# A two-block transformer kernel on one core: low part of the experts' gates by ScalarE, another place for the expert tiles, a fourth weight-row buffer

## The chip, the core and the metric

The kernel runs on one core of a Trainium2 chip. The metric is the device time of one execution in microseconds, smaller is better. A core has TensorE (PE in the profile; its weight loads are PEld), VectorE (DVE), ScalarE (ACT), GpSimd (POOL), and SyncE (SP), whose queue issues nearly all of the DMAs here.

## What is computed

The input is 256 tokens of width 1024. A first block of two layers is followed by a second block of two layers. Each layer of the first block has a mixer (attention, convolution and recurrence), then a mixture of 16,384 experts, then a gated per-layer embedding (PLE). The change lies in the experts' part, and its other edits touch what all parts share:

```python
def peer(xn, w_q, sub_keys, u, v):
    q = (xt @ w_q).reshape(t, 8, 2, 128)
    sc = jnp.einsum('thpc,pnc->thpn', q, sub_keys)
    top_s, top_i = lax.top_k(sc, 16)
    ...
    expert = i1 * 128 + i2                  # 8 heads x 16 experts for each token
    gate = jax.nn.softmax(best_s, axis=-1)
    act = jax.nn.gelu(jnp.einsum('cd,chkd->chk', xc, u[ec]))
    return jnp.einsum('chk,chkd->cd', gc * act, v[ec])
...
h = h + peer(rmsnorm(h, norm_ffn[l]), ...)
ple_gate = jax.nn.sigmoid(rmsnorm(h, norm_ple[l]) @ w_ple_gate[l])
h = h + ple_gate * (p[l] @ w_ple_proj[l])
```

## The kernel before

Nothing is gathered. For all 16,384 experts the kernel computes the product of the tokens with u (128 rows of experts on the partitions, 256 tokens as columns), applies gelu, multiplies by a dense table of gates that is zero for an expert that a token did not choose, and multiplies with v. The table `act` is [128, 128, 256] in float32, 128 KB of each partition. One step over u is a block `b` of 256 experts (64 blocks in a layer): four DMAs of 256 KB bring its rows into a `raw` buffer, VectorE turns them (L894, two transposes into `ut`) and TensorE makes 16 matmuls of 256 columns (L898). These matmuls in float32 stand in the trace as 32 records to a block. `u_split` is another form of this step, which the later blocks use: it turns the rows in place (L906) and splits them into a high and a low part. `u_out` applies gelu on ScalarE (L924, L927) and multiplies by the gates where they are already there (L925).

While the first u blocks run, the routing (scores, best 16, softmax of the gates) works on VectorE. Then comes the sweep, `spread_gates`, which builds the dense table for four tokens at a time: 64 groups in a layer, four of them to a block of u (`SWEEP_STEPS`). A group is

- `oh` (L859) and `eq` (L861): two comparisons of 128x512 on VectorE that give the one-hot rows of both halves of the expert's number. `oh` has two buffers, `eq` one.
- `rhs` (L863): one VectorE multiplication of 128x1024, `eq` times the gates `gp`. `gp` has two float16 parts, high and low, so that the sum of both holds the float32 gate. `rhs` has four buffers.
- 8 matmuls of 128x128 (L868): 4 tokens by two parts, into one PSUM bank out of three in turn.
- The evacuation: VectorE multiplies the experts for which u is already done (L872), ScalarE copies the other rows (L874).

After the sweep the v stage (`v_pair`) runs, in which TensorE does 24 matmuls of 512 columns for a pair of 128-expert rows (L943). Their stationary operands `ah` and `al` take over the buffers of `rhs` (same tag), their moving ones are the split rows of v, `whi` and `wlo`. Some of the u blocks run between them. The PLE follows; the load of its input p, `praw` (L993 is its transpose on TensorE), and the reload of `h` stand in SP's queue among the loads of its weights.

All rows of weights go through the ring of `raw` buffers (8 KB of a partition each, three of them). ScalarE rounds a part of them to `whi` (L167), and VectorE makes the rest `wlo` (L170), three buffers each, which TensorE reads. The order of each engine's instructions is set by the framework's scheduler, which walks the program by priorities and the buffers that are free: `K.ahead()` raises the priority of loads, `GPRIO` that of the sweep's matmuls. So another count of buffers or another duration of a step gives another order.

`SHIFTS` puts small unused tiles ahead of others, and thus moves what is allocated behind them. The entry "peer" puts 64 bytes of each partition between `act` and the tiles of the sweep.

Of the kernel before, what the change touches and what calls it, by code (L numbers as in the profile page):

```python
# [12 lines left out]
F32 = mybir.dt.float32  # L13
# [3 lines left out]
FP16 = mybir.dt.float16  # L17
U32 = mybir.dt.uint32
AF = mybir.ActivationFunctionType
ALU = mybir.AluOpType  # L20
# [4 lines left out]
S = 256  # L25
# [9 lines left out]
URGENT = 3000  # L35
SHIFTS = {"zp": (0, 288), "zp2": (384, 384), "ple": (384, 128), "peer": (64, 64)}
SQ_ACT = (2, 5, 7)
# [14 lines left out]
class Ctx:  # L52
# [21 lines left out]

    def shift(self, pool, size, name="shift"):

        if size:
            pool.tile([128, size // 4], F32, name=name, bufs=1)
# [78 lines left out]
    def raw_tile(self):  # L157
        return self.ring.tile([128, 2048], F32, name="raw", tag="raw", bufs=3)

# [515 lines left out]
GT = 4  # L675
GSCALE = 32768.0
# [9 lines left out]
def peer(K, a, l, pre, xg, row, pool, ctx):  # L686
# [8 lines left out]
    tc, nc = K.tc, K.nc  # L695
# [25 lines left out]
    nT = pool.tile([128, S], FP16, name="nT")  # L721
    gp = pool.tile([128, 2, S], FP16, name="gp")
    sc_b = [scratch([128, 4, 128]) for _ in range(2)]
# [82 lines left out]
    def routing():  # L806
# [24 lines left out]
        for src, dst in ((m_f, mT), (e_f, nT), (best_v.rearrange("p b h k -> p b (h k)"), None)):  # L831
# [3 lines left out]
            if dst is not None:  # L835
                nc.scalar.activation(dst, ps[:, 0:S], AF.Copy)
            else:
                rest = m_f.rearrange("p b n -> p (b n)")
                nc.scalar.activation(gp[:, 0], ps[:, 0:S], AF.Copy, scale=GSCALE)
                nc.vector.scalar_tensor_tensor(gp[:, 1], ps[:, 0:S], GSCALE, gp[:, 0], op0=ALU.mult,  # L840
                                               op1=ALU.subtract)
            yield
# [3 lines left out]
    def spread_gates():  # L846
# [5 lines left out]
        for i, t0 in enumerate(range(0, S, GT)):  # L852
# [8 lines left out]
            nc.vector.tensor_tensor(eq, io4, tok(nT), ALU.is_equal)  # L861
            rhs = pool.tile([128, 2, 128, GT], FP16, name="rhs", tag="rhs", bufs=4)
            nc.vector.tensor_tensor(rhs, eq[:, None].to_broadcast([128, 2, 128, GT]),  # L863
                                    gp[:, :, None, ts].to_broadcast([128, 2, 128, GT]), ALU.mult)
            with tc.high_priority(offset=GPRIO):
                for t in range(GT):
                    for part in range(2):
                        nc.tensor.matmul(pg[:, t], oh[:, :, t], rhs[:, part, :, t], start=t + part == 0,  # L868
                                         stop=t == GT - 1 and part == 1)
            pg = pg.rearrange("p t n -> p n t")  # L870
# [963 lines left out]
```

## Time and profile before

| | |
|---|---|
| three runs | 3617.34, 3620.2, 3631.05 us (median 3620.2) |
| profiled execution, its own time | 3630.35 us |
| its span in the trace | 3628.6 us |
| mean granted clock of TensorE | 0.975 |
| PE busy | 3484.8 us (96%) |
| PE weight loads busy | 3187.9 us (88%) |
| DVE busy | 2623.3 us (72%) |
| ACT busy | 1475.1 us (41%) |
| POOL busy | 604.2 us (17%) |
| sweep of layer 0, sweep of layer 1 | about 604 to 784 us, about 1922 to 2104 us |

The engines work side by side, so busy shares do not add up. "Granted clock" is the share of full speed at which TensorE was allowed to run, and a stretch at half of it lasts twice as long for the same matmuls. Where one engine waits, a row names the instruction that released it, after an arrow. "SPq" is SP's queue, with the DMAs that it issues.

### The profile page before, as it was taken

The page shows a single profiled execution, that of the slowest core. Times are in us where ns is not written, and L with a number is a line of the kernel's source. Part 1 is how long each engine was busy: PE and PEld are TensorE (multiplying, and loading weights), DVE is VectorE, ACT ScalarE, POOL GpSimd, SP SyncE. Part 2 cuts the span into 40 slices and gives each one's busy share as a digit, 9 for nine tenths or more (in the row PEclk, how much of TensorE's full clock was granted, in tenths as well). Part 3 has the DMA queues.
Part 4 walks back from the last instruction along what each step waited for, and adds up shares of the span by engine and source line. Part 5 has one row for each costly group of instructions (what it writes and reads, how often), then busy time and mean ns, then how long its engine had stood idle before and what let it go on. Part 6 is the DMA issues. An engine that isn't in the chain of part 4 may idle for free. (4 is left out here: it accounts for less than half of the span.)

```text
span 3628.6 us, 60192 instructions
## 1 busy us (share of the span) xinstructions
PE 3484.8 (96%) x23381; PEld 3187.9 (88%) x23381; DVE 2623.3 (72%) x4704; ACT 1475.1 (41%) x2418; POOL 604.2 (17%) x583
## 2 busy tenths in 40 slices
PE   8999998999999999999999999999989999999999
PEld 8898887888888889998888888888789899988999
DVE  6967668876666568775668866666578877698775
ACT  6455111234444446553112144444445344444434
POOL 1200111000000012101120000000033543345441
PEclk9999999999999999999999999999989999999999
DMA  7775756436666567765765346665666534665433
GB/s 178 180 187 140 164 128 139 93 94 189 184 184 187 196 156 173 196 159 147 155 138 113 94 130 190 188 189 186 190 151 141 109 85 116 164 129 120 96 85 126
DMA packets 433976, 541.70 MB, mean 149 GB/s; under 512 B 28665, under 2 KB 392219, under 8 KB 432667
## 3 DMA queue, kind: packets, MB, share of 16 engines
q1 hardware_dynamic: 433690, 537.86, 58.5%
q8 instruction: 183, 3.00, 0.4%
q14 instruction: 103, 0.84, 0.1%
HBM read 530.39 MB, written 6.32 MB: 148 GB/s over the span
## 5 line engine op out<-in xcount | busy, mean ns | idle before, releaser
L170 DVE TENSOR_TENSOR wlo<-raw,whi 128x1024 fp32r<-128x1024 f32 x670 | 862.7, 1293 | 325.8 <-ACT whi L167 311.3
L167 ACT ACTIVATE whi<-raw 128x1024 fp32r<-128x1024 f32 x696 | 728.7, 1051 | 709.0 <-PE mm L199 271.9
L898 PE MATMUL mm<-x,ut 128*128 128x256 f32 x2368 | 542.6, 386 | 1.2 <-ACT act L927 1.2
L200 PE MATMUL mm<-x,wlo 128*128 128x256 f32 x1760 | 506.6, 288 | 14.4 <-DVE wlo L170 14.1
L898 PEld LDWEIGHTS mm<-x,ut 128*128 128x128 f32 x2368 | 453.0, 194 | 64.3 <-ACT act L927 3.9
L198 PE MATMUL mm<-x,whi 128*128 128x256 f32 x1760 | 504.4, 287 | 3.3 <-ACT whi L167 3.3
L199 PE MATMUL mm<-x,whi 128*128 128x256 f32 x1708 | 488.9, 286 | 0.0
L200 PE MATMUL gg<-x,wlo 128*128 128x256 f32 (+1 forms) x1456 | 410.5, 282 | 9.3 <-DVE wlo L170 9.1
L198 PE MATMUL gg<-x,whi 128*128 128x256 f32 (+1 forms) x1456 | 410.9, 282 | 4.9 <-ACT whi L167 4.9
L199 PE MATMUL gg<-x,whi 128*128 128x256 f32 x1400 | 393.6, 281 | 1.3 <-DVE x L303 1.3
L200 PEld LDWEIGHTS mm<-x,wlo 128*128 128x128 f32 x1760 | 340.8, 194 | 18.2 <-DVE wlo L170 17.2
L198 PEld LDWEIGHTS mm<-x,whi 128*128 128x128 f32 x1760 | 340.7, 194 | 10.7 <-issue 5.6
L199 PEld LDWEIGHTS mm<-x,whi 128*128 128x128 f32 x1708 | 331.6, 194 | 1.9 <-issue 0.7
L943 PE MATMUL ax<-wlo,ah 128*128 128x512 f32 x1024 | 323.0, 396 | 2.6 <-DVE wlo L170 2.6
L943 PE MATMUL ax<-whi,al 128*128 128x512 f32 x1024 | 321.4, 395 | 0.0
L200 PEld LDWEIGHTS gg<-x,wlo 128*128 128x128 f32 (+1 forms) x1456 | 276.3, 190 | 11.7 <-DVE wlo L170 11.3
L943 PE MATMUL ax<-whi,ah 128*128 128x512 f32 x1024 | 286.6, 395 | 0.0
L198 PEld LDWEIGHTS gg<-x,whi 128*128 128x128 f32 (+1 forms) x1456 | 275.7, 189 | 8.2 <-ACT whi L167 5.6
L894 DVE STREAM_TRANSPOSE ut<-raw 128x1024 f32<-128x1024 f32 x148 | 181.9, 1236 | 130.8 <-DMA raw<-in_peer_u_dram 114.1
L199 PEld LDWEIGHTS gg<-x,whi 128*128 128x128 f32 x1400 | 265.9, 190 | 3.5 <-DVE x L303 1.4
L943 PEld LDWEIGHTS ax<-wlo,ah 128*128 128x128 f32 x1024 | 190.2, 187 | 54.8 <-DVE wlo L170 9.2
L943 PEld LDWEIGHTS ax<-whi,al 128*128 128x128 f32 x1024 | 191.7, 187 | 47.1
(534 smaller groups left out, 6593.5 us busy)
## 6 DMA issues: line engine op xcount, KB each, us to landing
raw<-in_w_in_dram SPq DMA_DIRECT2D x592, 256.0 KB
raw<-in_peer_u_dram SPq DMA_DIRECT2D x512, 256.0 KB
raw<-in_peer_v_dram SPq DMA_DIRECT2D x128, 1024.0 KB
raw<-in_w_branch_dram SPq DMA_DIRECT2D x16, 1024.0 KB
raw<-in_w_out_dram SPq DMA_DIRECT2D x16, 1024.0 KB
raw<-in_w_peer_q_dram SPq DMA_DIRECT2D x64, 256.0 KB
raw<-in_w_in_dram SPq DMA_DIRECT2D x64, 128.0 KB
raw<-in_w_branch_dram SPq DMA_DIRECT2D x32, 256.0 KB
```

Of the source, the lines that this page charges most:

```text
L167: nc.scalar.activation(view(hi), src, AF.Copy)
L170: (nc.gpsimd if pool else nc.vector).tensor_tensor(view(lo), src, view(hi).bitcast(F32), ALU.subtract)
L198: t.matmul(out, wh, xh, start=start, stop=False)
L199: t.matmul(out, wh, xl, start=False, stop=False)
L200: t.matmul(out, wl, xh, start=False, stop=stop)
L894: nc.vector.transpose(turned[jh], blk)
L898: nc.tensor.matmul(ps[:, jh], turned[jh][:, k].rearrange("p j c -> p (j c)"), xs[:, k], start=k + jh == 0, stop=k == KT - 1 and jh == 1)
L943: nc.tensor.matmul(out[tb][c], lhs[:, j, ts], r[:, c * 512:c * 512 + 512], start=b + j == 0 and lhs is ah and r is vh, stop=b == 63 and j ...
```

## The change

There are four edits.

1. The gates. `gp` now holds the high part alone, and a new tile `gl` the low part in float32. The multiplication by the gates is two steps: VectorE writes the high half of `rhs` (128x512 in place of 128x1024), and ScalarE writes the low half, with one activation of 128x128 for each of the four tokens, scaled by a column of `gl`. This half is now stored token by token, so that the matmul reads 128 elements that lie side by side. The matmuls are as many as before. VectorE's next `eq` must wait until ScalarE has read the one buffer of `eq`.
2. `SHIFTS["peer"]` becomes (0, 0). With this, and with `gp` 512 bytes smaller and `gl` 1024 bytes bigger, `oh`, `eq`, `rhs` (so `ah` and `al` too) and what follows lie 448 bytes further on, beside a common shift of 4096.
3. `raw` has four buffers in place of three (8 KB more).
4. The scratch for DMA descriptors is 4096 bytes in place of 8192.

```diff
-SHIFTS = {"zp": (0, 288), "zp2": (384, 384), "ple": (384, 128), "peer": (64, 64)}
+SHIFTS = {"zp": (0, 288), "zp2": (384, 384), "ple": (384, 128), "peer": (0, 0)}
...
-        return self.ring.tile([128, 2048], F32, name="raw", tag="raw", bufs=3)
+        return self.ring.tile([128, 2048], F32, name="raw", tag="raw", bufs=4)
...
-    gp = pool.tile([128, 2, S], FP16, name="gp")
+    gp = pool.tile([128, S], FP16, name="gp")
+    gl = pool.tile([128, S], F32, name="gl")
...
-                nc.scalar.activation(gp[:, 0], ps[:, 0:S], AF.Copy, scale=GSCALE)
-                nc.vector.scalar_tensor_tensor(gp[:, 1], ps[:, 0:S], GSCALE, gp[:, 0], op0=ALU.mult,
-                                               op1=ALU.subtract)
+                nc.scalar.activation(gp, ps[:, 0:S], AF.Copy, scale=GSCALE)
+                nc.vector.scalar_tensor_tensor(gl, ps[:, 0:S], GSCALE, gp, op0=ALU.mult, op1=ALU.subtract)
...
             eq = pool.tile([128, 128, GT], FP16, name="eq", tag="eq", bufs=1)
             nc.vector.tensor_tensor(eq, io4, tok(nT), ALU.is_equal)
-            rhs = pool.tile([128, 2, 128, GT], FP16, name="rhs", tag="rhs", bufs=4)
-            nc.vector.tensor_tensor(rhs, eq[:, None].to_broadcast([128, 2, 128, GT]),
-                                    gp[:, :, None, ts].to_broadcast([128, 2, 128, GT]), ALU.mult)
+            rhs = pool.tile([128, 2, 128 * GT], FP16, name="rhs", tag="rhs", bufs=4)
+            hi = rhs[:, 0].rearrange("p (n t) -> p n t", t=GT)
+            lo = rhs[:, 1].rearrange("p (t n) -> p t n", t=GT)
+            nc.vector.tensor_tensor(hi, eq, tok(gp), ALU.mult)
+            for t in range(GT):
+                nc.scalar.activation(lo[:, t], eq[:, :, t], AF.Copy, scale=gl[:, t0 + t:t0 + t + 1])
             with tc.high_priority(offset=GPRIO):
                 for t in range(GT):
-                    for part in range(2):
-                        nc.tensor.matmul(pg[:, t], oh[:, :, t], rhs[:, part, :, t], start=t + part == 0,
-                                         stop=t == GT - 1 and part == 1)
+                    nc.tensor.matmul(pg[:, t], oh[:, :, t], hi[:, :, t], start=t == 0, stop=False)
+                    nc.tensor.matmul(pg[:, t], oh[:, :, t], lo[:, t], start=False, stop=t == GT - 1)
...
-    nc = _bacc.Bacc("TRN2", target_bir_lowering=False, num_devices=1, dynamic_dma_scratch_size=8192)
+    nc = _bacc.Bacc("TRN2", target_bir_lowering=False, num_devices=1, dynamic_dma_scratch_size=4096)
```

The change also moves instructions, at places that the diff does not show. In the rows that follow, the lines of the kernel after lie up to three further on than before: L859 is now L860, L861 is L862, L863 is L866, L872 is L875, L874 is L877, L894 is L897, L906 is L909. "x2" stands for two like instructions in a row.

The first place is the beginning of layer 0's sweep, on VectorE, from the first multiplication by the gates on. Before:

```order
L863 TENSOR_TENSOR rhs<-eq,gp 128x1024
L861 TENSOR_TENSOR eq<-io_4654,nT 128x512
L863 TENSOR_TENSOR rhs<-eq,gp 128x1024
L894 STREAM_TRANSPOSE ut<-raw 128x1024
L861 TENSOR_TENSOR eq<-io_4654,nT 128x512
L863 TENSOR_TENSOR rhs<-eq,gp 128x1024
L861 TENSOR_TENSOR eq<-io_4654,nT 128x512
L863 TENSOR_TENSOR rhs<-eq,gp 128x1024
L894 STREAM_TRANSPOSE ut<-raw 128x1024
L872 SCALAR_TENSOR_TENSOR act<-act,gg 128x38x4
L859 TENSOR_TENSOR oh<-io_4654,mT 128x512
```

The same place on VectorE after:

```order
L866 TENSOR_TENSOR rhs<-eq,gp 128x512
L862 TENSOR_TENSOR eq<-io_4653,nT 128x512
L897 STREAM_TRANSPOSE ut<-raw 128x1024
L866 TENSOR_TENSOR rhs<-eq,gp 128x512
L862 TENSOR_TENSOR eq<-io_4653,nT 128x512
L866 TENSOR_TENSOR rhs<-eq,gp 128x512
L875 SCALAR_TENSOR_TENSOR act<-act,gg 128x38x4
L860 TENSOR_TENSOR oh<-io_4653,mT 128x512
L862 TENSOR_TENSOR eq<-io_4653,nT 128x512
L897 STREAM_TRANSPOSE ut<-raw 128x1024
L875 SCALAR_TENSOR_TENSOR act<-act,ax 128x38x4
L860 TENSOR_TENSOR oh<-io_4653,mT 128x512
```

Three groups' multiplications, no longer four, now stand ahead of the first evacuation, and the fourth group's comes only behind a transpose, a further evacuation and an `oh`. On ScalarE, at the same place after, the new activations stand between those that were there (L877 evacuations, L927 and L930 gelu):

```order
L841 ACTIVATE gp<-ax 128x256
L868 ACTIVATE rhs<-eq,gl 128x128 x12
L877 ACTIVATE act<-gg 128x90x4
L927 ACTIVATE mm<-mm 128x2x32
L868 ACTIVATE rhs<-eq,gl 128x128 x4
L877 ACTIVATE act<-ax 128x90x4 x2
```

The second place is the end of layer 0's sweep, on VectorE, where the first block of `u_split` has its two transposes. Before:

```order
L863 TENSOR_TENSOR rhs<-eq,gp 128x1024
L861 TENSOR_TENSOR eq<-io_4654,nT 128x512
L906 STREAM_TRANSPOSE raw<-raw 128x8x4x32 x2
L863 TENSOR_TENSOR rhs<-eq,gp 128x1024
L894 STREAM_TRANSPOSE ut<-raw 128x1024
L872 SCALAR_TENSOR_TENSOR act<-act,gg 128x64x4
L859 TENSOR_TENSOR oh<-io_4654,mT 128x512
L861 TENSOR_TENSOR eq<-io_4654,nT 128x512
L872 SCALAR_TENSOR_TENSOR act<-act,ax 128x64x4
L859 TENSOR_TENSOR oh<-io_4654,mT 128x512
L894 STREAM_TRANSPOSE ut<-raw 128x1024
L863 TENSOR_TENSOR rhs<-eq,gp 128x1024
```

The same place on VectorE after:

```order
L866 TENSOR_TENSOR rhs<-eq,gp 128x512
L897 STREAM_TRANSPOSE ut<-raw 128x1024
L862 TENSOR_TENSOR eq<-io_4653,nT 128x512
L909 STREAM_TRANSPOSE raw<-raw 128x8x4x32 x2
L875 SCALAR_TENSOR_TENSOR act<-act,ax 128x62x4
L860 TENSOR_TENSOR oh<-io_4653,mT 128x512
L866 TENSOR_TENSOR rhs<-eq,gp 128x512
L875 SCALAR_TENSOR_TENSOR act<-act,gg 128x62x4
L860 TENSOR_TENSOR oh<-io_4653,mT 128x512
L897 STREAM_TRANSPOSE ut<-raw 128x1024
L862 TENSOR_TENSOR eq<-io_4653,nT 128x512
```

The two transposes come about half a block of u earlier (the evacuation beside them has 62 rows of experts, before 64), and behind them stand an evacuation and an `oh` at once, where a multiplication and a transpose of 1.24 us came first.

The third place is SP's queue where layer 0's PLE begins. Before:

```order
L95 DMA raw<-in_peer_v_dram 128x2x1024 x21
L95 DMA raw<-in_w_ple_proj_dram 128x2x1024
L95 DMA raw<-in_w_ple_gate_dram 32x2x1024 x12
L95 DMA h<-h_store 128x2048
L95 DMA praw<-in_p_dram 128x2x256
L95 DMA raw<-in_w_ple_gate_dram 32x2x1024 x4
```

The same place on SP after:

```order
L96 DMA raw<-in_peer_v_dram 128x2x1024 x21
L96 DMA raw<-in_w_ple_proj_dram 128x2x1024
L96 DMA raw<-in_w_ple_gate_dram 32x2x1024 x16
L96 DMA h<-h_store 128x2048
L96 DMA praw<-in_p_dram 128x2x256
L96 DMA raw<-in_w_in_dram 32x8x256 x32
```

The last four loads of the gate's weights, 1 MB in all, have moved ahead of the loads of `h` and `praw`. In the same way four loads of `w_in` stand between the first two loads of norm vectors at the program's start, where they came behind all ten of these before. On the whole the other engines' orders differ from before in few places outside the sweep.

## Rows read from the trace of the kernel before

**Rows 1.** Busy time by stretch: both sweeps; columns in the first line.

```profile
core 0: us, PE busy (x) PEld busy (x) DVE busy (x) ACT busy (x) POOL busy (x), PEclk, DMA share, GB/s
604.00:784.00 180.00, 173.31 (x1006) 152.57 (x1006) 148.38 (x303) 38.14 (x95) 0.00 (x0) 0.96 0.39 91
1922.00:2104.00 182.00, 174.55 (x1008) 153.62 (x1007) 148.72 (x303) 38.24 (x95) 0.00 (x0) 0.95 0.39 90
```

**Rows 2.** PE's waits from 604 to 784: us, times, longest.

```profile
PE ax L868 <- DVE oh L859: 4.2, 3, 2.0
PE gg L868 <- DVE rhs L863: 1.6, 1, 1.6
```

**Rows 3.** PE's waits from 1922 to 2104, same columns.

```profile
PE ax L868 <- DVE oh L859: 4.9, 3, 2.8
```

**Rows 4.** Groups of VectorE, 604 to 784: count, busy us, mean ns, idle before.

```profile
L863 DVE TENSOR_TENSOR rhs<-eq,gp 128x1024 f16<-128x1024 f16 x64 | 43.7, 683 | 1.1
L894 DVE STREAM_TRANSPOSE ut<-raw 128x1024 f32<-128x1024 f32 x28 | 34.8, 1243 | 11.8 <-PE mm L898 7.9 <-DMA raw<-in_peer_u_dram 3.6
L861 DVE TENSOR_TENSOR eq<-io,nT 128x512 f16<-128x512 f16 x64 | 26.5, 413 | 0.8
L872 DVE SCALAR_TENSOR_TENSOR act<-act,ax 128x160 f32<-128x160 f32 (+15 forms) x42 | 15.0, 368 | 11.5 <-PE ax L868 11.3
```

**Rows 5.** A group of ScalarE, 604 to 784, same columns.

```profile
L874 ACT ACTIVATE act<-ax 128x352 f32<-128x352 f32 (+15 forms) x42 | 17.1, 420 | 62.8 <-DVE act L872 62.8
```

**Rows 6.** ScalarE by line: duration ns min/median/max, first and last start, form.

```profile
L1467 ACT ACTIVATE ddh<-packed,gt x64: 382/388/403, 2799.0 to 3458.7; 128x128 fp32r<-128x128 f32 x64
L302 ACT ACTIVATE x<-h,v_norm_mix x40: 491/497/512, 10.2 to 3146.0; 128x256 fp32r<-128x256 f32 x40
```

**Rows 7.** Timeline from the start: start us, length us, instruction, [idle before].

```profile
10.18 3.30 ACT L302 ACTIVATE x<-h,v_norm_mix 128x256 fp32r<-128x256 f32 x8
...
16.45 2.01 ACT L167 ACTIVATE whi<-raw 128x1024 fp32r<-128x1024 f32 x2 [2.36 <-DMA raw<-in_w_in_dram]
...
17.56 0.58 PE L198 MATMUL gg<-x,whi 128*128 128x256 f32 x1 [1.62 <-ACT whi L167]
```

**Rows 8.** Timeline, beginning of layer 0's sweep.

```profile
612.16 1.11 PE L868 MATMUL ax<-rhs,oh 128*128 128x128 f16 x8 [1.53 <-DVE oh L859]
```

**Rows 9.** Timeline, layer 0: a wait inside the sweep, then its end.

```profile
704.06 2.06 PE L868 MATMUL ax<-rhs,oh 128*128 128x128 f16 x16 [0.65 <-DVE oh L859]
...
755.90 2.37 DVE L906 STREAM_TRANSPOSE raw<-raw 128x1024 f32<-128x1024 f32 x2 [3.13 <-DMA raw<-in_peer_u_dram]
...
760.22 0.41 DVE L859 TENSOR_TENSOR oh<-io,mT 128x512 f16<-128x512 f16 x1
...
760.69 1.11 PE L868 MATMUL ax<-rhs,oh 128*128 128x128 f16 x8 [1.97 <-DVE oh L859]
...
763.42 0.88 PE L868 MATMUL gg<-rhs,oh 128*128 128x128 f16 x6 [1.62 <-DVE rhs L863]
```

**Rows 10.** Busy time by stretch, columns as in Rows 1: behind waits of PE.

```profile
613.50:621.00 7.50, 7.11 (x35) 5.56 (x33) 7.29 (x20) 2.34 (x5) 0.00 (x0) 0.55 0.53 116
705.50:710.00 4.50, 4.50 (x18) 3.77 (x16) 4.12 (x10) 1.01 (x3) 0.00 (x0) 0.62 0.71 146
...
764.00:768.00 4.00, 3.99 (x15) 3.15 (x14) 3.86 (x10) 0.94 (x3) 0.00 (x0) 0.62 0.72 255
...
2082.00:2088.00 6.00, 5.99 (x20) 4.73 (x20) 5.79 (x13) 0.94 (x3) 0.00 (x0) 0.50 0.50 175
```

**Rows 11.** The same, for two stretches of the mixers.

```profile
160.00:260.00 100.00, 98.97 (x842) 97.83 (x841) 73.98 (x184) 50.64 (x78) 4.57 (x2) 1.00 0.75 191
1500.00:1600.00 100.00, 100.00 (x873) 97.31 (x872) 68.67 (x122) 49.51 (x88) 3.56 (x2) 1.00 0.68 178
```

**Rows 12.** The same, line L943 alone: only PE, PEld, clock, DMA.

```profile
1200.00:1300.00 100.00, 100.00 (x430) 80.14 (x429) 1.00 0.56 188
```

**Rows 13.** PE's waits over the whole span, columns as in Rows 2.

```profile
PE mm L993 <- DMA praw<-in_p_dram: 14.2, 2, 8.5
```

## The prediction, made before the changed kernel had run

> **What bounds the kernel now.** I read the busy times by stretch first, since the change works mostly in the two sweeps. There TensorE is busy 173.31 of 180 us and 174.55 of 182 us, VectorE 148.38 and 148.72, ScalarE 38.14 and 38.24 [rows 1]. A sweep has 64 groups, so a group takes 173.31/64 = 2.71 us of TensorE (its own matmuls and a quarter of a block of u), 2.32 us of VectorE and 0.60 us of ScalarE. TensorE is the bound, VectorE is close behind, ScalarE has room. The reader is to see that lighter work for VectorE can win only the time in which TensorE waits for it. That is 6.7 us in the first sweep and 7.45 us in the second (180 or 182 less busy time), and most of it is for `oh` or `rhs`: 4.2 and 1.6 us, and 4.9 us for `oh` in the second [rows 2, 3].
>
> The second thing that a wait costs is the clock. Behind the waits TensorE's granted clock falls from full speed (2.4 GHz) towards half of it (1.2 GHz): 0.55 over 7.5 us, 0.62 over 4.5 us, 0.62 over 4 us in layer 0 [rows 10]. What is lost is the length times one minus the clock. Over whole sweeps that is 180 x 0.04 = 7.2 us and 182 x 0.05 = 9.1 us [rows 1]. So the most that the sweeps can give back is 6.7 + 7.45 + 7.2 + 9.1 = 30 us of 3630, or 0.8%.
>
> **The gates' multiplication, steady part.** VectorE's step of 128x1024 took 683 ns, and its steps of 128x512 take 413 ns [rows 4]. The change makes the first into one of the second kind: 64 x 0.27 = 17.3 us less VectorE time in each sweep, 131 us in place of 148. This lies beside TensorE's 173 us and is worth nothing by itself.
>
> What it adds is four activations of 128x128 a group on ScalarE. No such step is in the trace of before. The nearest row is a 128x128 activation with a multiplier that differs by partition, 388 ns [rows 6]. One of 128x256 takes 497 ns alone [rows 6], but eight in a row take 3.30 us, 0.41 us each [rows 7]. So one overlaps the next by 0.09 us, and I take 0.30 us each in a row and 0.39 apart. That is 1.2 to 1.55 us a group, 77 to 99 us a sweep. ScalarE goes from 38 to 115 to 137 us, still under 173.
>
> The cost is in the chain, since `eq` has one buffer: `eq` (0.41), a hand-over (`oh` ended at 760.63 and TensorE began at 760.69, 0.06 us [rows 9]), four activations (1.2 to 1.55), a hand-over, the next `eq`. That is 1.73 to 2.08 us. If ScalarE has one other step in front, as its evacuation of 0.42 us [rows 5], it is 2.15 to 2.5 us. All this is below 2.71 us, so TensorE should stay the bound; the other VectorE steps (transpose, `oh`, the evacuation) stand between one `eq` and the next and hide part of it. I take 0 for the steady part.
>
> The Trainium skill speaks against this edit: "ScalarE: Activation LUTs", in Rules for kernel authors, says to use VectorE and not ScalarE for multiplications, VectorE being up to about three times faster in 16-bit types. No run here shows that ratio for this step. By that rule, if ScalarE's time counted in full, the edit would cost and not gain; the second rival is this case.
>
> **The beginning of the sweep.** Before, TensorE waited 1.53 us for the fourth group's `oh` [rows 8]; the fourth multiplication was done long before. After, that multiplication stands behind a transpose (1.24 us [rows 4]), an evacuation (0.37) and an `oh` (0.41). Walking the new order with these durations, the fourth group is ready some 0.7 us later than before, and each of the next two groups has a wait of about 1 us where it had little or none, while the first groups lose nothing. So TensorE arrives at its next ten matmuls of u 1 to 1.6 us later. For both layers I take **+3 us**, with 0 and +4 as ends.
>
> **The end of the sweep.** Two transposes of `u_split` waited 3.13 us for their DMA and ended at 758.27 [rows 9]. Behind them stood a multiplication, a transpose, an evacuation and then the `oh` that TensorE waited for, done at 760.63: 2.36 us. In the new order only an evacuation (0.37) and an `oh` (0.41) stand there, so it is ready 1.6 us sooner, and the wait of 1.97 us shrinks to about 0.4. The next wait, 1.62 us for `rhs`, stood behind the other transpose; now the multiplication goes ahead of it. In layer 1 the first of the two is 2.8 us, the longest of its 4.9 [rows 3]; the second I take as in layer 0. The clock behind them costs 4 x 0.38 = 1.5 us in layer 0 and 6 x 0.50 = 3.0 us in layer 1 [rows 10]. All of it: 1.6 + 1.6 + 2.4 + 1.6 + 1.5 + 3.0 = 11.7 us. But the transposes now come half a block earlier, and if their DMA doesn't, the wait for it (3.13 us) stands ahead of other groups. The fourth `raw` buffer lets these DMAs be issued up to a block earlier. I take two thirds, **-8 us**, ends -12 and +3.
>
> **Inside the sweep.** A wait of 0.65 us [rows 9] and the clock after it (4.5 x 0.38 = 1.7 us [rows 10]) stand in layer 0, and I take layer 1 as alike: 4.7 us. With 17 us less on VectorE it should go, but the order is new in every block and may have such a place elsewhere. I take **-3 us**, ends -5 and +6.
>
> **The fourth weights' buffer outside the sweep.** At the start four loads of `w_in` (1 MB) now stand ahead of most norm vectors. The first rounding of `w_in` waited 2.36 us for its load and TensorE's first product started at 17.56 [rows 7], so these come earlier; but the scaled x (from 10.18 on [rows 7]) waits for vectors that now come later. I take 0, ends -3 and +3. At the PLE `praw` is queued behind four more loads of 256 KB, and TensorE already waits 14.2 us for `praw` in the two layers [rows 13]. One more buffer lets those four go out one buffer sooner, which should leave `praw` where it was: 0, with 0 and +8 as ends. Elsewhere TensorE reads `whi` and `wlo`, of which there are as many as before. The smaller scratch for descriptors costs nothing that the profile can show, since SP's queue issues these DMAs.
>
> **The other place of `oh`, `rhs`, `ah`, `al`.** No row shows what a place costs. But the same form of matmul runs at two paces with TensorE never short of work: 98.97 us for 842, 117.5 ns each, in one layer's mixer, and 114.5 ns in the other's [rows 11]. In the v stage a matmul of 512 columns takes 100/430 = 232.6 ns [rows 12], where 512 columns at 2.4 GHz are 213.3 ns. The v stages have 3072 of these. Twice the difference between the paces of 256 columns, 6 ns, would be 18 us; all that lies above 213.3 ns would be 59 us. The stationary operands `ah` and `al` move by 448 bytes beside all others. The place may matter or not, and to either side; unchanged is likeliest: 0, with -59 to +18 as ends.
>
> By the Trainium skill, "SBUF — State Buffer", Who interferes with whom, TensorE never waits on another engine's access there. By that sentence this term would be 0; the two paces in the trace are no contradiction, as they don't show what causes them.
>
> **The sum.** +3 - 8 - 3 = -8 us against the profiled execution (3630.35 us, 1.75 us of it outside the span). That execution lies 10 us above the median of the runs, and I put the same gain there: 3620.2 - 8 = **3612 us**.
>
> **Rivals.** First, the new place of `ah` and `al` makes the v stage faster by one such step: 3612 - 18 = 3594 us, and less if by more. For it speaks that 232.6 ns is 9% above the columns' own time while nothing is waited for; against it, that no row ties a pace to a place. Second, ScalarE's chain becomes the bound of the sweep. It decides when the way from `eq` to `eq` is over 2.71 us. With two other steps of 0.42 us in front and 0.39 us for each activation it is 2.08 + 0.84 = 2.92 us, 0.21 us over, and 128 groups make 27 us: 3612 + 27 = 3639 us, more if the clock falls too. For it speaks the single buffer of `eq`; against it, that ScalarE now idles 62.8 us of a sweep ahead of one group of its steps alone [rows 5], and that the groups don't all meet it so. Third, the place makes the v stage slower: 3612 + 18 = 3630 us. Fourth, the edit moves nothing: the waits at the sweep's ends stand where they were, for the DMA or for the transposes, and the time is 3620 us.
>
> **How the numbers follow.** The forecast has 0.42, the first rival 0.28, the second 0.14, the third 0.08, the fourth 0.08. A measurement of this kernel tells about 0.5% from no change, 18 us: faster is under 3602, slower over 3638. The forecast's own range, 3598 to 3622, lies a quarter in "faster" (0.1); the first rival is nearly all faster (0.26). The second is slower for three quarters (0.11), the third for a third (0.03). This makes 0.36 faster, 0.50 same, 0.14 slower. For the range I leave out a tenth on each side, the deep end of the first rival and the upper half of the second: 3580 to 3638 us.
>
> **What would show it.** VectorE's busy time in a sweep near 131 us and ScalarE's at 115 to 137 us, with TensorE's idle time below 6.7 us, would show the steady part right. The two waits at the end should be under 1 us, those at the beginning longer. Rows in which VectorE waits at `eq` for ScalarE's activation, and TensorE behind it, would show the second rival. 430 matmuls in 100 us of the v stage would show that the place doesn't matter. I would be wrong if these counts change, or if `praw` is waited for longer.

## The result and the profile after

The changed kernel takes 3587.76 us (median of 4 runs, 3581.54 to 3594.85) against 3624.15 us for the kernel before, with one more run of it. The ratio is 0.990, with a 95% interval from 0.987 to 0.993: 36 us or 1.0% less. The prediction said 3612 us with a range of 3580 to 3638, and had "same", that is within 0.5%, as the likeliest case. The time lies in the range, but it moved more than four times as far as the sum said (36 us, not 8).

The profiled execution of after has a span of 3593.1 us (before 3628.6). Its busy times in the two sweeps, with the columns of Rows 1:

```profile
core 0: us, PE busy (x) PEld busy (x) DVE busy (x) ACT busy (x) POOL busy (x), PEclk, DMA share, GB/s
602.00:764.00 162.00, 155.76 (x995) 137.79 (x992) 127.07 (x294) 111.59 (x344) 0.00 (x0) 0.97 0.38 93
1906.00:2070.00 164.00, 157.39 (x996) 138.73 (x994) 127.47 (x294) 111.86 (x345) 0.00 (x0) 0.96 0.39 92
```

Against [rows 1] the sweeps are some 15 us shorter each. VectorE has 127 us of work, about what was forecast (131), ScalarE 112 (115 to 137 forecast; three of the 64 groups lie ahead of the window). But TensorE's own busy time fell too, from 173 to 156 us with nearly as many matmuls in the window (995, before 1006), and its idle time hardly: 6.2 us, before 6.7. So TensorE was not merely waited for less; its work became shorter. Its waits in the first sweep, as in [rows 2]:

```profile
PE ax L871 <- DVE rhs L866: 2.0, 2, 1.1
PE ax L871 <- DVE oh L860: 1.5, 1, 1.5
PE gg L871 <- DVE rhs L866: 1.2, 1, 1.2
PE gg L871 <- DVE oh L860: 0.9, 1, 0.9
```

VectorE's groups from 602 to 764, as in [rows 4], and ScalarE's new group:

```profile
L866 DVE TENSOR_TENSOR rhs<-eq,gp 128x512 f16<-128x512 f16 x61 | 25.6, 420 | 0.8
L862 DVE TENSOR_TENSOR eq<-io,nT 128x512 f16<-128x512 f16 x61 | 25.0, 410 | 6.8 <-ACT rhs L868 6.2
```

```profile
L868 ACT ACTIVATE rhs<-eq,gl 128x128 f16<-128x128 f16 x246 | 80.9, 400 | 38.9 <-DVE eq L862 22.2 <-PE ax L872 12.0 <-PE gg L872 4.2
```

The multiplication went from 683 to 420 ns, and `eq` now waits for ScalarE, 6.2 us in the first sweep.

The sweep's matmuls by line: duration in ns (min, median, max), first and last start, form. First before, where all eight of a group are L868; then after, where L871 reads the high half (four tokens' elements side by side, so one token's are 8 bytes apart) and L872 the low half (one token's 128 elements side by side). Both are the moving operand; the stationary one, `oh`, is read with jumps of 8 bytes in every kernel here:

```profile
L868 PE MATMUL ax<-rhs,oh x672: 274/297/303, 609.3 to 2102.7; 128*128 128x128 f16 x168
```

```profile
L871 PE MATMUL ax<-rhs,oh x336: 273/278/314, 603.0 to 2067.5; 128*128 128x128 f16 x168
L872 PE MATMUL ax<-rhs,oh x336: 237/238/299, 603.1 to 2067.6; 128*128 128x128 f16 x168
```

A duration holds the way through the array, and the pace is in the starts. Two groups in the timeline of after (start, length):

```profile
641.01 0.28 PE L871 MATMUL ax<-rhs,oh 128*128 128x128 f16 x1
641.11 0.24 PE L872 MATMUL ax<-rhs,oh 128*128 128x128 f16 x1
641.18 0.28 PE L871 MATMUL ax<-rhs,oh 128*128 128x128 f16 x1
...
642.34 0.24 PE L872 MATMUL ax<-rhs,oh 128*128 128x128 f16 x1
642.41 3.89 PE L901 MATMUL mm<-x,ut 128*128 128x256 f32 x17
```

From 641.01 to 642.41 are 16 matmuls, 87.5 ns each; over both sweeps the mean between starts, outside stretches at the half clock, is about 89 ns, and 117 before. The two sweeps have 1024 of them: 1024 x 28 ns is some 28 us.

The pace before does not follow TensorE's clock, either. These eight matmuls of before ran in a stretch at the lower of its two levels (granted clock 0.50) and took 1.11 us, as the eight at full clock did [rows 8]; the first line is from the timeline, the second its stretch with L868 alone (only PE, PEld, clock, DMA):

```profile
615.71 1.11 PE L868 MATMUL ax<-rhs,oh 128*128 128x128 f16 x8 [0.39 <-DVE rhs L863]
615.60:616.90 1.30, 1.11 (x8) 0.83 (x8) 0.50 1.10 228
```

In such stretches of before the sweep's matmuls keep a median step of 118 ns, while the records of u's go from 216 to 427. So it was not that clock that set their pace. It also means that a stretch at half clock does not make every matmul last twice as long, as was said ahead of the prediction.

The second place where the time fell is the routing ahead of each sweep. First before, then after, busy time by stretch:

```profile
401.00:608.00 207.00, 196.46 (x927) 171.75 (x926) 149.17 (x523) 28.73 (x65) 42.67 (x56) 0.99 0.68 147
```

```profile
409.00:601.00 192.00, 192.00 (x921) 169.79 (x921) 142.19 (x512) 31.85 (x72) 42.55 (x56) 1.00 0.68 150
```

TensorE no longer idles there. The third place goes the other way: the v stage of layer 0, before and after.

```profile
786.00:1305.00 519.00, 517.26 (x2865) 442.93 (x2863) 338.38 (x332) 240.93 (x277) 0.00 (x0) 1.00 0.62 185
```

```profile
764.00:1285.00 521.00, 509.80 (x2866) 445.22 (x2864) 338.78 (x333) 241.34 (x278) 0.00 (x0) 1.00 0.63 184
```

It is 2 us longer, though TensorE is busy 7.5 us less: its matmuls of 512 columns are faster (227.8 ns apart, before 234.3), and the time so won is spent waiting (11.2 us idle, before 1.7).

The table adds the stages of both layers in the profiled execution of each kernel (us, from the trace's first instruction to the last matmul's end). A stage runs from the start of its first matmul to that of the next stage's; the v stage ends with its last matmul, the PLE with the last product of its gate. The other columns are the experiments of the next section.

| stage | before | after | gates only | buffer only | place only | gates and place | low half interleaved |
|---|---|---|---|---|---|---|---|
| mixers | 771.7 | 787.2 | 765.8 | 781.5 | 767.4 | 767.2 | 778.6 |
| u with routing | 411.4 | 385.9 | 409.6 | 386.8 | 411.8 | 407.0 | 385.9 |
| sweeps | 355.8 | 326.2 | 326.5 | 348.8 | 355.2 | 327.5 | 345.7 |
| v stages | 1037.8 | 1042.5 | 1037.1 | 1051.0 | 1027.5 | 1025.2 | 1045.6 |
| PLE | 98.4 | 100.7 | 101.3 | 100.4 | 98.6 | 101.3 | 100.8 |
| second block | 947.7 | 944.4 | 941.3 | 947.6 | 939.7 | 940.7 | 941.8 |
| sum | 3622.9 | 3586.9 | 3581.6 | 3616.2 | 3600.3 | 3568.8 | 3598.4 |

The second block is little touched by any of these, and yet varies by 8 us. A difference of that size in one profiled execution is thus nothing to explain; the verdicts below go by the medians of several runs, beside runs of the kernel before.

### The profile page after: what moved, and what is told of

It is laid out like the page before. It is cut to its first block, busy times and chain, and to the rows that moved or that the text cites. A ratio compares the mean times of both kernels' runs of the same rounds, so it can differ in the third digit from the quotient of the medians.

```text
span 3593.1 us, 60732 instructions
## 1 busy us (share of the span) xinstructions
PE 3446.7 (96%) x23381; PEld 3175.7 (88%) x23381; DVE 2586.9 (72%) x4704; ACT 1624.7 (45%) x2928; POOL 602.3 (17%) x583
## 5 line engine op out<-in xcount | busy, mean ns | idle before, releaser
L201 PE MATMUL mm<-x,wlo 128*128 128x256 f32 x1760 | 505.8, 288 | 25.5 <-DVE wlo L171 14.2
L946 PE MATMUL ax<-whi,ah 128*128 128x512 f32 x1024 | 279.3, 390 | 0.1
L897 DVE STREAM_TRANSPOSE ut<-raw 128x1024 f32<-128x1024 f32 x148 | 182.5, 1237 | 88.2 <-PE mm L901 64.5
```

Source lines behind the costliest of these rows:

```text
L201: t.matmul(out, wl, xh, start=False, stop=stop)
L897: nc.vector.transpose(turned[jh], blk)
L946: nc.tensor.matmul(out[tb][c], lhs[:, j, ts], r[:, c * 512:c * 512 + 512], start=b + j == 0 and lhs is ah and r is vh, stop=b == 63 and j ...
```

## The experiments

**Each part alone.** The theory after the result had three parts: the layout of the low half sets TensorE's pace in the sweeps; the fourth buffer ends the idle time in the routing; the place sets the pace of the v stage, whose gain is lost again in waits. The rival for the sweeps was the prediction's own, that VectorE's relief is what counts.

The gates' edit alone, as a diff against the changed kernel:

```diff
-SHIFTS = {..., "peer": (0, 0)}
+SHIFTS = {..., "peer": (64, 64)}
-    ... name="raw", tag="raw", bufs=4)
+    ... name="raw", tag="raw", bufs=3)
-    ... dynamic_dma_scratch_size=4096)
+    ... dynamic_dma_scratch_size=8192)
```

> The kernel before with the gates' edit alone (low half by ScalarE, stored token by token); place, buffers and scratch as before. Pace theory: TensorE reads a half that lies side by side faster, so the sweep's matmuls go from 116.8 ns to about 90 ns apart, each sweep is some 14 us shorter, and the time falls by 25 to 30 us to about 3596 us. Wait theory (the prediction's): the matmuls stay at 117 ns and only waits and clock in the sweeps shrink, by 5 to 12 us, to about 3614 us.

It took 3588.11 us against 3626.21, ratio 0.9903 (0.9882 to 0.9925): as much as the whole change. The sweeps are 326.5 us, 29 less than before, the matmuls 88 ns apart, and that pace alone explains them: 1024 x 28 ns. TensorE's idle time in the sweeps did not fall (15.2 us in both, before 14.1). The wait theory falls as the main cause.

The fourth buffer with the smaller scratch alone, as a diff against the kernel before:

```diff
-    ... name="raw", tag="raw", bufs=3)
+    ... name="raw", tag="raw", bufs=4)
-    ... dynamic_dma_scratch_size=8192)
+    ... dynamic_dma_scratch_size=4096)
```

> The kernel before with the fourth weights' buffer and the smaller descriptor scratch alone. Buffer theory: VectorE no longer waits for rows of u during the routing (53.6 us of waiting before in layer 0), TensorE's 10.5 and 7.5 us of idle time there go to about 0, and the time falls by 10 to 14 us to about 3611 us. Rival (the prediction's): the buffer moves nothing, 3624 us within 5, and TensorE's idle time in the routing stays at 10 us.

It took 3623.01 us, ratio 0.9988 (0.9975 to 1.0002): the time of neither theory's full form. The routing went as the buffer theory said, 25 us shorter over both layers, with TensorE never idle:

```profile
408.00:601.00 193.00, 193.00 (x929) 170.69 (x928) 144.12 (x508) 29.41 (x65) 42.59 (x56) 1.00 0.67 149
```

VectorE's wait for rows of u in the first routing, before (401 to 608) and with the buffer alone (406 to 600):

```profile
DVE ut L894 <- DMA raw<-in_peer_u_dram: 53.6, 12, 9.5
DVE ut L894 <- DMA raw<-in_peer_u_dram: 5.8, 2, 3.8
```

But the mixers are 10 us longer, the v stages 13 and the PLE 2 (the table). So this edit is a gain of 31 us (sweeps too) and a loss of 25, and its result near zero is a balance.

The place alone, against the kernel before:

```diff
-SHIFTS = {..., "peer": (64, 64)}
+SHIFTS = {..., "peer": (0, 0)}
```

> The kernel before with SHIFTS peer at (0, 0) alone. Place theory: the v stage's matmuls of 512 columns go from 234 to 228 ns apart, but the split rows of v and u come no faster, so TensorE idles 8 to 10 us more in each v stage, whose length stays at 519 to 521 us: time within 5 us of before. Rival: the pace is worth what it says, 3072 x 6 ns = 20 us less, 3604 us. Second rival: the place sets no pace, 234 ns stays.

It took 3611.03 us, ratio 0.9964 (0.9952 to 0.9976), 13 us less by the ratio. The pace went from 234.3 to 228.9 ns (the durations' median from 394 to 389), with no instruction changed and TensorE's in the same order: so the place sets it. Of what these matmuls read, only `ah` and `al` moved, but all else that lies behind `act` moved with them, so that it is their own place is likely and not shown. My expectation that all of it is given back was wrong: 10 us stay in the v stages. That is one half to two thirds of 3072 x 5.4 = 16.6 us.

The other way round, the changed kernel with the old place:

```diff
-SHIFTS = {..., "peer": (0, 0)}
+SHIFTS = {..., "peer": (64, 64)}
```

> The changed kernel with SHIFTS peer back at (64, 64). Place theory: 512-column matmuls are back at 234 ns, TensorE's idle time in a v stage falls from 11 to about 2 us, and the time stays within 5 us of the changed kernel's 3588 us. Rival (the pace counts in full): 3608 us. Sweep as in the changed kernel, 160 to 164 us.

It took 3593.21 us, ratio 0.9912 (0.9892 to 0.9931), about 5 us above the changed kernel by the medians, though the intervals overlap; its v stages are 5.6 us longer (1048.1). The pace is back at 233.5 ns and TensorE's idle time in the v stages falls from 21.7 to 10.2 us, more than I had said remains. With four buffers, about two thirds of the pace's gain (3072 x 5.7 ns = 17.5 us) end in waiting.

**What the fourth buffer costs.** With four buffers, the v stage of after has this place (timeline: start, length, idle before):

```profile
2186.45 1.07 PE L946 MATMUL ax<-whi,ah 128*128 128x512 f32 x4
...
2186.65 1.06 ACT L912 ACTIVATE whi<-raw 128x1024 fp32r<-128x1024 f32 x1 [1.59 <-PE ax L946]
...
2187.27 2.37 DVE L909 STREAM_TRANSPOSE raw<-raw 128x1024 f32<-128x1024 f32 x2 [3.75 <-DMA raw<-in_peer_u_dram]
...
2190.14 2.35 DVE L913 TENSOR_TENSOR wlo<-raw,whi 128x1024 fp32r<-128x1024 f32 x2
2191.40 0.19 PEld L201 LDWEIGHTS mm<-x,wlo 128*128 128x128 f32 x1 [2.04 <-DVE wlo L913]
2191.40 0.39 PE L201 MATMUL mm<-x,wlo 128*128 128x256 f32 x1 [1.84 <-DVE wlo L913]
```

VectorE stands 3.75 us at the two transposes (L909) of the next block of u, whose rows are still on their way, and the `wlo` (L913) of the block that TensorE is at stands behind them in its queue. My reading is that the buffer lets the scheduler put these transposes earlier, and that the rows don't come earlier by as much. TensorE's waits in the first v stage are these, 10.9 us in all:

```profile
PE mm L201 <- DVE wlo L913: 5.5, 4, 2.5
PE gg L201 <- DVE wlo L913: 5.4, 6, 1.6
```

The gates' edit and the place, without the fourth buffer, should then be better than the whole change (a diff against the changed kernel, as are those that follow):

```diff
-    ... name="raw", tag="raw", bufs=4)
+    ... name="raw", tag="raw", bufs=3)
-    ... dynamic_dma_scratch_size=4096)
+    ... dynamic_dma_scratch_size=8192)
```

> The changed kernel with three weights' buffers and the 8192-byte scratch again: gates' edit and place alone. If the fourth buffer gives back in the mixers and the v stages (6 us each) more than it wins in the routing, and the place is worth its 15 us, this is faster than the changed kernel: about 3575 us, with TensorE idle 9 us in each routing and 2 to 5 us in each v stage. If the fourth buffer carries a part of the gain, it is slower: about 3600 us.

It took 3579.06 us, ratio 0.9879 (0.9855 to 0.9904). The intervals of this and of the changed kernel overlap, so the 8 us between the medians are likely, not certain; the stages show where they are: mixers 20 and v stages 17 us less than after, the routing 21 us more. In the first v stage the wait for `wlo` of u is gone:

```profile
766.00:1277.00 511.00, 509.27 (x2863) 444.15 (x2863) 338.40 (x332) 241.39 (x278) 0.00 (x0) 1.00 0.64 187
```

A last doubt was that the fourth buffer also moves all that lies behind it. Three buffers, with an unused tile ahead:

```diff
-        self.shift(self.ring, 64)
+        self.shift(self.ring, 64 + 8192)
-    ... name="raw", tag="raw", bufs=4)
+    ... name="raw", tag="raw", bufs=3)
```

> The changed kernel with three weights' buffers, and an unused 8 KB tile ahead of them, so that all that is behind them lies where the changed kernel has it (scratch 4096). If the fourth buffer costs time in the mixers and v stages by the order that comes with it, this kernel is like e2_gates_place: 3579 us, v stages 511 to 514 us. If the cost is the place of what lies behind, it has the mixers and v stages of the changed kernel (521 us) and the routing of before: about 3600 us.

It took 3585.7 us, ratio 0.9888 (0.9868 to 0.9908): between the two expectations, and not apart from either by its interval. The stages are clearer: mixers 766.8 and v stages 1028.8 us, as in gates and place (whose order of instructions it has), and routing 410.1. So what the fourth buffer loses in those stages comes with the order, not with the place. It is no scatter either: the mixers take 779 to 787 us in all five kernels here with four buffers, and 766 to 774 in all nine with three. Why the mixers lose, I did not follow to a row.

**Layout or engine.** ScalarE does the low half as in the changed kernel, but writes it in the old layout:

```diff
-            lo = rhs[:, 1].rearrange("p (t n) -> p t n", t=GT)
+            lo = rhs[:, 1].rearrange("p (n t) -> p t n", t=GT)
```

> The changed kernel, but ScalarE writes the low half in the order of before (the four tokens' elements side by side). Pace theory: the matmuls are back at 117 ns apart, each sweep at 174 to 177 us, time about 27 us above the changed kernel: 3615 us. Wait theory (the gain is VectorE's relief): sweeps stay at 162 to 164 us and the time at 3588 us.

It took 3607.05 us, ratio 0.9954 (0.9937 to 0.9971), 19 us above the changed kernel. The matmuls of the low half are as before:

```profile
L872 PE MATMUL ax<-rhs,oh x336: 293/297/303, 600.6 to 2080.7; 128*128 128x128 f16 x168
```

They are 116.9 ns apart, with TensorE's and ScalarE's instructions in the same order as in the changed kernel. So the layout alone is the pace, and it is worth 19 to 20 us (sweeps 345.7 against 326.2). Less than the 27 us expected, since TensorE waits less when it is slower: 8.6 us of idle time in the sweeps against 12.8. (ScalarE's activations are slower too when they write with jumps, 0.56 us in place of 0.40, but with TensorE's idle time smaller this held nothing up.) This kernel also shows what VectorE's relief and the order give without the pace: 355.8 - 345.7 = 10 us in the sweeps. The prediction's term for that was 8 us. (The fourth buffer is in it: alone it gives 7.)

The layout without ScalarE: VectorE writes the low half too.

```diff
-            for t in range(GT):
-                nc.scalar.activation(lo[:, t], eq[:, :, t], AF.Copy, scale=gl[:, t0 + t:t0 + t + 1])
+            nc.vector.tensor_tensor(lo.rearrange("p t n -> p n t"), eq, tok(gl), ALU.mult)
```

(`gl` is float16 here, as the low part of `gp` was.)

> The changed kernel, but VectorE writes the low half (128x512, gates' low part in float16 as before), token by token, and ScalarE nothing. Pace theory: the matmuls stay at 90 ns; VectorE has one more step of 128x512 a group (0.42 to 0.69 us), 2.5 us or more a group against TensorE's 2.4 to 2.5, so it becomes the bound: sweeps of 165 to 185 us, time 3592 to 3625 us. Rival: with VectorE burdened, the matmuls too are at 117 ns again.

It took 3811.4 us, ratio 1.0506 (1.0485 to 1.0528), far over the range that I gave. The matmuls stayed fast (87 ns), but VectorE's step is far longer than the 0.42 to 0.69 us that I expected:

```profile
L867 DVE TENSOR_TENSOR rhs<-eq,gl x128: 2392/2430/2465, 594.7 to 2285.6; 128x512 f16<-128x512 f16 x128
```

It reads side by side and writes with jumps of 256 bytes, and this costs 2.43 us where the same step without jumps is 0.42, about a sixth of it. So the layout is out of reach in this form on VectorE: the other engine is what makes the layout cheap.

**The other half.** Gates and place, with the high half too stored token by token, by VectorE in the same form:

```diff
-            hi = rhs[:, 0].rearrange("p (n t) -> p n t", t=GT)
+            hi = rhs[:, 0].rearrange("p (t n) -> p n t", t=GT)
```

> Gates' edit and place with three buffers, and the high half too stored token by token by VectorE. Pace theory: the matmuls fall further, to 65 to 80 ns apart, 5 to 10 us a sweep for TensorE; if VectorE writes 128x512 with jumps as fast as before (0.42 us), the time is 10 to 20 us below e2_gates_place. If that step takes 0.7 us or more, VectorE bounds the sweep, and the time is at or above e2_gates_place.

It took 3764.14 us, ratio 1.0387 (1.0364 to 1.041), for the same reason (VectorE 2436 ns). But the matmuls are now 56 to 58 ns apart, both lines alike:

```profile
L871 PE MATMUL ax<-rhs,oh x336: 216/219/314, 605.2 to 2237.6; 128*128 128x128 f16 x168
```

128 columns at 2.4 GHz are 53.3 ns. So before, at 117 ns, each of these matmuls took twice the time of its columns, because of the jumps in the moving operand, and the changed kernel has mended one half of that.

VectorE can walk in the order of the output instead, reading with jumps of 8 bytes and writing side by side:

```diff
-            nc.vector.tensor_tensor(hi, eq, tok(gp), ALU.mult)
+            nc.vector.tensor_tensor(hi.rearrange("p n t -> p t n"), eq.rearrange("p n t -> p t n"),
+                                    gp[:, ts][:, :, None].to_broadcast([128, GT, 128]), ALU.mult)
```

> Gates' edit and place with three buffers; VectorE writes the high half too token by token, but walks in the order of the output (reads with jumps, writes side by side). Pace theory: matmuls at 58 ns apart as in e2_both_side. If only the writes with jumps are slow on VectorE, this step takes 0.55 to 0.75 us in place of 2.44 us, VectorE has some 2.35 to 2.5 us a group, and the sweeps are 150 to 165 us: time 3555 to 3585 us. If reads with jumps are as slow, the time is 3750 us again.

It took 3577.54 us, ratio 0.9867 (0.9844 to 0.989), the same as gates and place. The step is 0.69 us:

```profile
L866 DVE TENSOR_TENSOR rhs<-eq,gp x128: 648/686/695, 598.9 to 2048.7; 128x512 f16<-128x512 f16 x128
```

TensorE is then faster than VectorE can feed it: it idles 16 us in each sweep, before 7. The gain went into a new wait.

GpSimd is idle in the sweeps. The same step there:

```diff
-            nc.vector.tensor_tensor(hi, eq, tok(gp), ALU.mult)
+            nc.gpsimd.tensor_tensor(hi.rearrange("p n t -> p t n"), eq.rearrange("p n t -> p t n"),
+                                    gp[:, ts][:, :, None].to_broadcast([128, GT, 128]), ALU.mult)
```

> The same, with the high half written by GpSimd, which is idle in the sweeps, in the order of the output. Pace theory: 58 ns; if GpSimd takes under 2.2 us for 128x512 and VectorE is not slowed by it, VectorE has 1.7 us a group and the sweeps fall to about 150 us, time about 3550 us. If GpSimd takes 2.4 us or more it bounds the sweep: 64 groups by its time, 3580 us and above.

It took 3559.61 us, ratio 0.9809 (0.9786 to 0.9831), the best of all: 1.9% below the kernel before, and below the changed kernel. GpSimd's step by line, and the first sweep, which is now 153 us:

```profile
L866 POOL TENSOR_TENSOR rhs<-eq,gp x128: 1040/1048/1352, 601.8 to 2038.3; 128x512 f16<-128x512 f16 x128
```

```profile
604.00:757.00 153.00, 143.43 (x995) 123.89 (x994) 107.48 (x233) 117.87 (x346) 67.06 (x63) 0.94 0.44 103
```

VectorE has 107 us of work, TensorE 143 of 153, and still 9.6 us of waiting. The last run asked whether `eq`'s single buffer is at fault:

```diff
-            eq = pool.tile([128, 128, GT], FP16, name="eq", tag="eq", bufs=1)
+            eq = pool.tile([128, 128, GT], FP16, name="eq", tag="eq", bufs=2)
```

> e3_hi_pool with two buffers for eq. If the single buffer (VectorE waits for ScalarE's and GpSimd's reads of eq) is what holds VectorE back in the sweeps, TensorE's idle time there falls from 9.5 us to 6 or less and the time by 5 to 10 us to about 3552 us. If the idle time stands at the sweep's beginning and end for other reasons, the time stays within 4 us of 3560 us.

It took 3580.96 us, ratio 0.9873 (0.985 to 0.9895), 21 us more than with one buffer. VectorE's waits for `eq`'s readers did shrink (from 10.0 us for ScalarE to 2.7 in the first sweep):

```profile
DVE eq L862 <- ACT rhs L869: 2.7, 4, 1.0
```

But TensorE's waits grew:

```profile
PE gg L872 <- DVE oh L860: 6.0, 5, 3.2
PE ax L872 <- DVE oh L860: 5.2, 7, 2.3
```

It idles 13.4 us in a sweep (with one buffer 9.6), and the sweep takes in one more block of u. What holds `oh` up shows in its own duration, first with one buffer, then with two:

```profile
L860 DVE TENSOR_TENSOR oh<-io,mT x128: 381/418/1324, 600.6 to 2039.9; 128x512 f16<-128x512 f16 x128
L860 DVE TENSOR_TENSOR oh<-io,mT x128: 373/788/1296, 597.4 to 2044.1; 128x512 f16<-128x512 f16 x128
```

The comparison takes 0.41 us by itself. With two buffers 80 of the 128 start while GpSimd's multiplication runs, with one buffer 20, and nearly all of these are stretched: the long ones (over 0.45 us, 76 and 15 of them, and 12 of `eq` with two buffers) all end 0.28 us after GpSimd's step has ended. So VectorE's comparison, once it has started beside GpSimd's step, does not end before it, and the new order puts four times as many of `oh` there: `oh` and `eq` together take 159 us of VectorE, with one buffer 116. The single buffer was not what held the sweeps up, and neither expectation had it that two would hurt. Why layer 1's mixer and the PLE are slower as well (by some 6 us together), I did not follow.

## Why the prediction was right and wrong

The time lies in the range and the sign is right, but the likeliest case was not what happened. By the prediction's own steps:

**What bounds the kernel.** Right that TensorE bounds the sweeps. Wrong was the ceiling drawn from it, 30 us as the sum of waits and lost clock. It held TensorE's own 173 us as given, and the change makes them 156.

**The steady part.** VectorE (127 us, 131 forecast), ScalarE (112; one activation 0.397 us alone, 80.9/246 = 0.33 in a row, 0.30 to 0.39 forecast) and the chain through `eq` (6.2 us of waiting in the first sweep) were sized right, and the second rival did not come. ScalarE's four activations take 1.3 us a group where VectorE's multiplication takes 0.42, and yet they cost nothing, since ScalarE had the time. The failed step is one that the sum left out: the diff turns what TensorE reads from elements 8 bytes apart into elements side by side, I had even written that down in the description of the change, and gave the matmuls no new price because their number stayed. It was worth 19 us by the medians (low half interleaved, against after), and some 28 us of the sweeps, by its pace, where the gates' edit stood alone. The trace of before could have raised the question: the 16 matmuls that start at 704.06 take 2.06 us, of which the last is 0.297 long, so 15 steps are 1.76 us [rows 9]: 117.5 ns each, over twice the 53.3 ns of their 128 columns, with TensorE not waiting.

The Trainium skill has the rule that bears on this: "SBUF — State Buffer", in Specifications, says that SBUF is read in lines of 16 bytes, that at least two hits in a line are needed for full bandwidth, and that each step to a new line has a penalty. If two hits were enough, the old layout (two float16 elements of a token in each 16 bytes) would already be at full pace; the trace does not agree, since two elements a line gave 117 ns and eight a line 56 to 58. That fewer steps to a new line are faster agrees with the trace. The measurement decides.

**Beginning, inside and end of the sweep.** The sum was -8 us for waits and clock together, and the kernel with the old layout and the rest of the change shows -10. But the buffer alone shows -7 in the sweeps, and with the gates' edit alone TensorE's idle time there did not fall. So most of the -10 comes with the fourth buffer, whether by rows of u that arrive in time or by the order, and little from the lighter multiplication, to which I had given it: that the sum came near is in good part luck. The price of the clock was also too high where the sweep's own matmuls ran at half clock, since those of before lost nothing there (118 ns at either level). Term by term, in layer 0 of after: at the beginning TensorE waits 1.20, 1.08 and 0.95 us for the next multiplications (L866), 3.2 us in all, before 1.9: near the half of the +3 that the walk had given to each layer. The wait inside is gone, as forecast. At the end the 1.97 and 1.62 us have become 1.5 and 0.9, less of a gain than I took.

**The fourth buffer outside the sweep.** I took 0, and alone it measured -3 by the medians (ratio 0.9988, its interval holds 1). The number was right for a wrong reason. I had looked only at the waits by name at the start and the PLE, not at TensorE's idle time in the routing: 10.5 us in layer 0, which busy time by stretch would have given (196.46 of 207, above). VectorE stood 53.6 us there at rows of u that were not there yet, and TensorE waited for routing steps behind it. The buffer ends that, and its order costs nearly as much in the mixers and the v stages. Together with the other two edits it is a loss by the medians, 3587.8 against 3579.1 us, though within the intervals. `praw`, which I feared to see later, is waited for 7.5 us in both layers together, before 14.2 [rows 13].

**The place.** The first rival had the mechanism right: the place of the expert tiles, most likely of `ah` and `al`, sets the pace of the v stage; why it does, no run shows. Its size, 6 ns a matmul and 18 us in all, is near what was found alone (5.4 ns, 13 us). I gave it 0.28 and "unchanged" the most; no row of before could tell. In the changed kernel about 5 us of it remain. That the measured time stayed in the range owes much to the depth that this rival had lent it, though its main cause was another.

So the 36 us are, by the experiments: about 19 from the layout, about 10 from waits and clock in the sweeps (most of it with the fourth buffer), some 25 in the routing from the fourth buffer, about 5 from the place, and against these some 20 us or more lost in mixers and v stages by the order that comes with the fourth buffer. These parts overlap and don't add exactly.

## What to carry to other kernels

Price a matmul by the pace of its starts against its columns before anything else: where it is far above the columns at the granted clock with nothing waited for, the way its operands lie is the first suspect, and a change that only re-sorts an operand is a change of TensorE's time. An idle or half-idle engine can pay for the better layout where the busy one can't. An idle engine is free only as long as it does not hold up a busy one: look at the durations of steps that run side by side. One more buffer is also another order of the whole program, so read each stage, not the sum.

## What the runs showed of the hardware

- The same matmul (stationary 128x128, moving 128x128, float16) is started every 117 ns when the moving elements are 8 bytes apart and every 56 to 58 ns when they lie side by side (before, and the four runs that store both halves so). Alternating the two gives 87 to 89 ns. The stationary elements were 8 bytes apart in all of them.
- At a granted clock of 0.50 the first kind keeps its 118 ns (before), the second goes from 56 to 107 ns (both halves side by side, written by GpSimd or by VectorE in the order of the output), and the float32 matmuls of u go from 216 to 427 ns between their records' starts.
- A VectorE multiplication of 128x512 in float16 takes 0.42 us with all side by side, 0.69 us reading with jumps of 8 bytes and with one factor repeated along the row, and 2.43 us writing with jumps of 256 bytes. GpSimd takes 1.05 us for the second of these.
- A VectorE comparison of 128x512 with two inputs (0.41 us) that started while this GpSimd step ran ended 0.28 us after it, in up to 1.3 us (one and two buffers of `eq`).
- A ScalarE activation of 128x128 from float16 with a multiplier by partition takes 0.397 us reading with jumps of 8 bytes and writing side by side, and 0.560 us with jumps in both (low half interleaved).
- With the stationary operand (and what lies behind it) 448 bytes further on, beside 4096 in common, matmuls of 512 columns went from 234 to 228 ns; 64 bytes less did the same (229 ns, place alone), and 512 bytes more left it at 234 (gates only).
